# An encoder's step from out-projection to feed-forward: other h buffers, gate and up operands made earlier

## The chip, the cores and the metric

The kernel runs on one core of one Trainium2 chip. The metric is the device time of one execution in microseconds (us). The engines are TensorE (PE in the rows; PEld is its weight load), VectorE (DVE), ScalarE (ACT), GpSimd (POOL) and SyncE (SP), whose queue issues most of the DMAs.

## The reference

One layer of an encoder, for a prompt of 1024 tokens and a sample of 256, all in float32, with D = 1024 and a feed-forward width of 2816:

```python
x = x + token_mixer(rms_norm(x, norm_mix_g), w_in, ..., w_out)       # Fourier mixing and latent attention, then @ w_out
x = x + (silu(n @ w_gate) * (n @ w_up)) @ w_down   # n = rms_norm(x, norm_ffn_g)
return rms_norm(x, final_norm_g)
```

## The kernel before, in words

Activations lie transposed, features on the partitions. The 1280 tokens are three chunks: t = 0 and t = 1 (512 prompt tokens each) and t = 2 (the 256 of the sample). Each float32 operand of a product is split into a high and a low part: ScalarE makes the high one by a rounding copy (line 93), and a subtraction on DVE or POOL makes the low one (line 98). One block product is then three matmuls (`mm3`, line 112). All engines but SP run the instructions in the order in which the code is written; SP's DMAs are placed by a scheduler.

The stage around the change has two parts.

The **out-projection** (`out_proj`) multiplies the mixed heads by `w_out`, eight blocks m = 0..7 of 128 output features. For t < 2 a block is 48 matmuls of 256 columns, for t = 2 it is 24. A first loop does t = 0 beside the last of the attention. A second loop does t = 1 in step m and t = 2 two steps later. After each block DVE adds the residual (line 1100: the sum h), ScalarE squares it (1081), and POOL adds up the squares (1082, `hacc`). When a chunk is through, `Rstd` makes 1/rms: `pre` splits `hacc` (`ssq`; ScalarE and DVE), `mid` sums over the partitions by two matmuls with ones (188, 189) and takes Ln and Exp on ScalarE (197, 199), `post` refines in four DVE steps (208 to 215; the first is `var`, the last gives `rstd`). `scaled` then multiplies h by gain and rstd (1111: c). The sum h of t < 2 is kept in four `h` tiles, each for two blocks m and both chunks, and is stored to DRAM after t = 1. Tiles of the tag "w" (nine buffers of 8 KB a partition) hold h, split weights (`whl`), split gate and up operands (`wo`) and others.

The **feed-forward** multiplies pairs of 128-feature blocks of `w_gate` and `w_up` with the two prompt chunks by a seven-product scheme (Strassen's). The weight side has four plain blocks (A11, A12, A21, A22) and four sums (S1 to S4). The chunk side has B11 and B21 (from t = 0), B22 and T3 (from t = 1 alone at first), and the combinations T1, T2, T3, T4. `prep(upto)` makes the next weight-side pieces in the order of the list `seq`, and `run(n)` does product n: 24 matmuls. `rest(n)` multiplies a plain piece with the sample chunk: 12 matmuls. For the first pair (fp = 0) the order of `seq` is A11, A12, A21, A22 for gate and up (n = 0 to 7), then S2, S1, S3, S4 and A22 again (n = 8 to 17). Of the plain pieces, A11 and A12 are also multiplied with prompt chunks, as run(0) to run(3). From fp = 1 on the order is a steady one.

In `before` the calls stand so: after the second loop `prep(4)`, run(0), run(1); post of chunk 1 and eight `scaled`; pre of chunk 2; run(2); mid of chunk 2; `prep(8)`; the T1, T2, T4 combinations; run(3); the `rest` products; the later runs, each with its `prep` and `split_block` ahead of it. All low parts of gate and up pieces are POOL's.

Of the kernel before, what the change touches and what calls it, by code (L numbers as in the profile page):

```python
# [35 lines left out]
def encoder_kernel(ctx, tc, A, out):  # L36
# [22 lines left out]
    def wtile(shape, dt, s="w"):  # L59
        return sb.tile(shape, dt, tag="w", bufs=n_w, name=nm(s))  # L60
# [1006 lines left out]
    def hview(m, t):  # L1067
        if (m, t) in HV:
            return HV[m, t]
        if t < 2:  # L1070
            return Ha[m // 2][:, m % 2, t * 512 : (t + 1) * 512]
        return Hb[0][:, m, :]

    def square_sum(acc, m, t):
# [11 lines left out]
    def load_res(m, t):  # L1086
        t0, n = TC[t]
        xres[m, t] = araw([P, n])
        nc.sync.dma_start(xres[m, t], A["x"][m * P : (m + 1) * P, t0 : t0 + n])

    def out_proj(w, m, t):
        n = TC[t][1]
        b = bank()
        for c in range(8):
            mm3(b[:, :n], (w[:, 0, c * P : (c + 1) * P], w[:, 1, c * P : (c + 1) * P]), MX[c, t], c == 0, c == 7)
        if t == 0 and m % 2 == 0:
            Ha[m // 2] = wtile([P, 2, 1024], F32, "h")
        elif t == 2 and m == 0:
            Hb[0] = wtile([P, 8, 256], F32, "hb")
        nc.vector.tensor_tensor(hview(m, t), b[:, :n], xres.pop((m, t)), op=ALU.add)  # L1100
        square_sum(hacc, m, t)
        if t == 1:
            nc.sync.dma_start(hd[m], Ha[m // 2][:, m % 2, :])
        elif t == 2 and m == 7:
            nc.sync.dma_start(hd2, Hb[0])

# [52 lines left out]
    for m in range(10):
        W.split(min(io + 8 + m + 2, idn))  # L1160
        if m < 8:
            load_res(m + 1, 1) if m < 7 else None
            out_proj(W.get(io + 8 + m), m, 1)
        if m == 7:
            hch[1] = Rstd(hacc[1], 512, D)
            hch[1].pre()
        if m > 0 and m < 9:
            load_res(m - 1, 2)
        if m == 9:
            hch[1].mid()  # L1170
        if m > 1:
            out_proj(W.get(io + 6 + m), m - 2, 2)
            plain2(m - 2)
        if m == 0:
            hch[0].mid()
            hch[0].post()
        elif m < 5:
            chunk0(m - 1)
            chunk0(m + 3)
        for k in {4: (0,), 5: (1,), 6: (2, 3), 7: (4,), 8: (5, 6), 9: (7,)}.get(m, ()):  # L1180
            parts0(k)
# [17 lines left out]
    def prep(upto):  # L1199


        while done[0] < min(upto, len(seq)):
            n = done[0]
            fp, k, name = seq[n]
            q = 2 * fp + k
            load_pair(q)
            ra, rb = raws2[q]
            blk = {"A11": ra[:, :512], "A12": ra[:, 512:], "A21": rb[:, :512], "A22": rb[:, 512:]}
            blk |= {"S3": blk["A11"], "S1": blk["A21"], "S4": blk["A12"], "S2": sums.get(q)}
            eng = nc.vector if fp else nc.gpsimd  # L1210
# [26 lines left out]
    def rest(n):  # L1237

        fp, k, name = seq[n]
        if name not in FIRST:  # L1240
            return
        st, L = state[fp, k], piece[n]
        if name == "A11":
            st["G"] = bank()
        i, h = int(name[1]) - 1, int(name[2]) - 1
        R = [HN[4 * h + j, 2] for j in range(4)]

        block_product(st["G"][:, i * 256 : (i + 1) * 256], L, R, name == "A11", i == 1 or h == 1, i == 1)
        if name == "A22":
            g = st["2"] = tmp([P, 2, 256])  # L1250
# [112 lines left out]
    split_block("T3", nc.vector)
    run(8)
    run(9)
    split_block("B22", nc.vector)
# [251 lines left out]
```

## Time and the profile before

| | us |
|---|---|
| median of 3 runs (1469.0 to 1472.6) | 1472.11 |
| the profiled execution's own time | 1468.22 |
| its span, first to last instruction | 1466.4 |
| TensorE busy | 1405.7 (96%) |
| DVE, POOL, ACT busy | 851.7, 638.8, 558.7 |

The profile is of one execution, so its parts add up to 1466.4 and not to the median. A busy TensorE may still run at a lower clock: the granted clock (1.00 is 2.4 GHz, 0.50 is 1.2 GHz) has a column of its own in the view of stretches.

### The profile page before, as it was taken

How to read it: one execution, taken by the hardware profiler on the slowest of the kernel's cores; microseconds unless marked ns; L12 is line 12 of the kernel's file. 1: busy time of each engine (PE TensorE's matmuls, PEld its weight loads, DVE VectorE, ACT ScalarE, POOL GpSimd, SP SyncE). 2: the span in 40 equal slices, each digit the busy share in tenths (PEclk: the TensorE clock that was granted, in tenths of full speed). 3: DMA queues.
4: the chain of work that ended last, by engine and by line, in shares of the span. 5: the costliest groups of instructions: out<-in, count | busy, mean ns of one | idle time of the engine just before them, and what ended most of it. 6: DMA issues, size and time to landing. Idle time of an engine off the chain costs nothing.

```text
span 1466.4 us, 27581 instructions
## 1 busy us (share of the span) xinstructions
PE 1405.7 (96%) x11096; PEld 1357.0 (93%) x11096; DVE 851.7 (58%) x1279; ACT 558.7 (38%) x1115; POOL 638.8 (44%) x456
## 2 busy tenths in 40 slices
PE   9998899999989998889999999999999999999996
PEld 8898797888879998789999999999999999999996
DVE  6867947898994755863243324333432467777334
ACT  5544346776763433532222221222123331112134
POOL 3456514453552555664435443434343142325233
PEclk9999999999999998999999999999999999999998
DMA  8103445686764562031212122212222552243012
GB/s 261 50 1 118 135 130 131 152 201 171 187 187 118 180 201 85 8 114 47 78 66 92 47 72 74 83 48 73 80 74 93 176 166 84 85 149 135 1 43 103
DMA packets 75041, 157.51 MB, mean 107 GB/s; under 512 B 13088, under 2 KB 23072, under 8 KB 74784
## 3 DMA queue, kind: packets, MB, share of 16 engines
q1 hardware_dynamic: 71856, 150.74, 33.8%
q10 hardware_dynamic: 2736, 3.95, 0.7%
q8 instruction: 87, 1.43, 0.4%
q0 software_dynamic: 320, 1.05, 0.2%
q14 instruction: 42, 0.34, 0.1%
HBM read 99.57 MB, written 35.16 MB: 92 GB/s over the span
## 4 chain that ended last, share of the span: by engine, by line
PE 80%; DVE 7%; issue 3%; ACT 2%; POOL 2%; DMA 1%; SPq 1%; DVEq 0%; ACTq 0%; POOLq 0%
PE mm L112 50%; PE sc L112 23%; PE sc L744 1%; PE sc L745 1%; PE sc L748 1%; PE sc L747 1%; PE sc L746 1%; DVE b L98 1%; DVE mx L755 1%; DVE c L1338 1%; PE mm L821 1%; DVE pt L98 1%; SPq L805 0%; POOL wo L98 0%; DVE at L98 0%
## 5 line engine op out<-in xcount | busy, mean ns | idle before, releaser
L112 PE MATMUL sc<-b,wo 128*128 128x256 f32 x2288 | 299.2, 282 | 15.8 <-ACT wo L93 7.7
L112 PE MATMUL mm<-at,whl 128*128 128x256 f32 x2640 | 304.9, 277 | 4.6 <-DVE h L1412 2.3
L112 PEld LDWEIGHTS mm<-at,whl 128*128 128x128 f32 x2640 | 302.8, 188 | 6.0 <-DVE h L1412 2.9
L112 PEld LDWEIGHTS sc<-b,wo 128*128 128x128 f32 x2288 | 282.2, 193 | 17.3 <-ACT wo L93 8.3
L98 POOL TENSOR_TENSOR wo<-wraw,wo 128x512 fp32r<-128x512 f32 x156 | 211.8, 1380 | 160.2 <-ACT wo L93 160.1
L1269 DVE TENSOR_TENSOR e<-e,sc 128x512 f32<-128x512 f32 x64 | 44.0, 688 | 223.6 <-PE sc L112 223.6
L1412 DVE TENSOR_TENSOR h<-h,mm 128x512 f32<-128x512 f32 (+1 forms) x192 | 111.7, 595 | 102.6 <-PE mm L112 101.9
L98 POOL TENSOR_TENSOR whl<-wraw,whl 128x1024 fp32r<-128x1024 f32 (+3 forms) x49 | 117.5, 2410 | 89.5 <-ACT whl L93 78.2
L112 PE MATMUL mm<-hn,wo 128*128 128x256 f32 x1056 | 130.3, 277 | 0.0
L112 PE MATMUL mm<-b,wo 128*128 128x256 f32 x1056 | 127.1, 276 | 0.6 <-POOL wo L98 0.6
L112 PEld LDWEIGHTS mm<-hn,wo 128*128 128x128 f32 x1056 | 125.0, 188 | 0.0
L112 PEld LDWEIGHTS mm<-b,wo 128*128 128x128 f32 x1056 | 123.1, 188 | 1.0 <-POOL wo L98 0.8
L112 PEld LDWEIGHTS mm<-mx,whl 128*128 128x128 f32 x960 | 112.8, 189 | 2.3 <-POOL whl L98 1.5
L112 PE MATMUL mm<-mx,whl 128*128 128x256 f32 x960 | 113.6, 279 | 1.1 <-POOL whl L98 0.9
L93 ACT ACTIVATE at<-araw 128x512 fp32r<-128x512 f32 x55 | 32.9, 625 | 161.2 <-DMA araw<-a 97.8
L93 ACT ACTIVATE wo<-wraw 128x512 fp32r<-128x512 f32 x156 | 87.8, 619 | 10.1 <-POOL wraw L1213 5.7
L112 PE MATMUL mm<-pt,vt 128*128 128x512 f32 (+1 forms) x324 | 84.8, 398 | 4.3 <-DVE pt L98 3.9
L98 POOL TENSOR_TENSOR wo<-tmp,wo 128x512 fp32r<-128x512 f32 x22 | 29.2, 1325 | 132.8 <-ACT wo L93 132.8
L1425 POOL TENSOR_TENSOR h<-h,araw 128x512 f32<-128x512 f32 (+1 forms) x24 | 27.4, 1147 | 136.0 <-DVE h L1412 90.8
L98 POOL TENSOR_TENSOR pt<-wraw,pt 128x512 fp32r<-128x512 f32 x40 | 60.1, 1502 | 51.1 <-ACT pt L93 40.9
L1082 POOL TENSOR_TENSOR hacc<-hacc,tmp 128x512 f32<-128x512 f32 (+1 forms) x35 | 42.8, 1223 | 84.0 <-ACT tmp L1081 80.6
L112 PE MATMUL mm<-cn,whl 128*128 128x256 f32 x585 | 73.6, 282 | 5.2 <-DVE qw L581 3.2
(198 smaller groups left out, 2277.9 us busy)
## 6 DMA issues: line engine op xcount, KB each, us to landing
Y<-P SPq DMA_DIRECT2D x160, 128.0 KB, 2.5
wraw<-in_w_gate SPq DMA_DIRECT2D x22, 512.0 KB, 3.7
wraw<-in_w_up SPq DMA_DIRECT2D x22, 512.0 KB, 4.1
wraw<-in_w_down SPq DMA_DIRECT2D x22, 512.0 KB, 3.7
araw<-a SPq DMA_DIRECT2D x44, 256.0 KB, 4.6
a<-e SPq DMA_DIRECT2D x42, 256.0 KB, 2.0
araw<-in_x SPq DMA_DIRECT2D x32, 256.0 KB, 4.6
wraw<-in_w_out SPq DMA_DIRECT2D x16, 512.0 KB, 3.7
```

What stands on the lines that cost most here:

```text
L93: nc.scalar.activation(o, i, AF.Copy)
L98: eng.tensor_tensor(o, i, f(hi), op=ALU.subtract)
L112: nc.tensor.matmul(o[:, c], L[a], R[b][:, c], start=first and i == 0 and j == 0, stop=end, skip_group_check=again)
L744: nc.tensor.matmul(o, qn[0][:, cs], k[0], start=True, stop=False)
L745: nc.tensor.matmul(o, qn[0][:, cs], k[1], start=False, stop=False)
L746: nc.tensor.matmul(o, qn[1][:, cs], k[0], start=False, stop=False)
L747: nc.tensor.matmul(o, qr[0][:, cs], krst[kt], start=False, stop=False)
L748: nc.tensor.matmul(o, qr[1][:, cs], krst[kt], start=False, stop=True)
L1082: nc.gpsimd.tensor_tensor(acc[t], acc[t], q, op=ALU.add)
L1269: add = lambda o, x, y: nc.vector.tensor_tensor(o, x, y, op=ALU.add)
L1412: nc.vector.tensor_tensor(hview(m, t), hview(m, t), o, op=ALU.add)
L1425: nc.gpsimd.tensor_tensor(HV[m, t], HV[m, t], hres.pop((m, t)), op=ALU.add)
```

## The change

The sum h of t < 2 gets one tile for four blocks m of one chunk, and each block is stored as soon as it is added, 16 stores of 256 KB for eight of 512 KB. The second loop does t = 2 one step after t = 1, splits `w_out` one block further ahead, and makes the first pair's eight plain gate and up pieces in its steps 6 and 7; their low parts are DVE's. The first sums of the gate weights (S3, S1, S2, now S4 too) stand in step 7 on POOL. The rest is written in another order, the T4 differences move to POOL, and ScalarE loads the table set with Ln and Exp right after the feed-forward loop.

```diff
-            Ha[m // 2] = wtile([P, 2, 1024], F32, "h")
+        if t < 2 and m % 4 == 0:
+            Ha[t, m // 4] = wtile([P, 4, 512], F32, "h")
...
-        if t == 1:
-            nc.sync.dma_start(hd[m], Ha[m // 2][:, m % 2, :])
+        if t < 2:
+            nc.sync.dma_start(hd[m][:, t * 512 : (t + 1) * 512], hview(m, t))
...
-            if name == "S2":
+            if name == "S2" and q not in sums:
                 made("S3", "A11", "A21", ALU.subtract)
                 made("S1", "A21", "A22", ALU.add)
                 blk["S2"] = sums[q] = tmp([P, 512])
                 made("S2", "A22", "S3", ALU.subtract)
+                if fp == 0:
+                    made("S4", "A12", "S2", ALU.subtract)
...
-            piece[n] = split((o[:, 0], o[:, 1]), blk[name], nc.gpsimd)
+            piece[n] = split((o[:, 0], o[:, 1]), blk[name], nc.gpsimd if n > 7 else nc.vector)
...
+    LNEXP = "natural_log_exp_and_others"
+    for m in range(9):
+        W.split(min(io + 8 + m + 3, idn))
+        if m == 6:
+            prep(4)
+        if m == 7:
+            prep(8)
+        if m < 8:
+            load_res(m + 1, 1) if m < 7 else None
+            load_res(m, 2)
+            out_proj(W.get(io + 8 + m), m, 1)
+        if m == 7:
+            hch[1] = Rstd(hacc[1], 512, D)
+            hch[1].pre()
+            prep(9, True)
+        if m == 8:
+            hch[1].mid()
+        if m > 0:
+            out_proj(W.get(io + 7 + m), m - 1, 2)
+            plain2(m - 1)
...
+        for k in {4: (0,), 5: (1,), 6: (2,), 7: (3, 4, 5, 6, 7)}.get(m, ()):
+            parts0(k)
+        if m == 5:
+            load_pair(0)
+            load_pair(1)
+    hch[1].post()
...
-    prep(4)
     run(0)
-    run(1)
-    hch[1].post()
     for j in range(4):
         B["T3"][j], B["B22"][j] = low(vtile([P, 512], F32, "c")), low(vtile([P, 512], F32, "c"))
         scaled(B["T3"][j][1], j, 1)
         scaled(B["B22"][j][1], j + 4, 1)
+    run(1)
     hch[2] = Rstd(hacc[2], 256, D)
     hch[2].out = r2
     hch[2].pre()
-    run(2)
-    hch[2].mid()
-    prep(8)
+    prep(10)
...
-        combine(t4r[:, j], C0.pop(j + 4), B["T2"][j][1])
+        nc.gpsimd.tensor_tensor(t4r[:, j], C0.pop(j + 4), B["T2"][j][1], op=ALU.subtract)
+    hch[2].mid()
+    run(2)
+    run(3)
     split_block("T2", nc.vector)
-    run(3)
...
+    nc.scalar.preload_act_table_set(LNEXP)
```

On TensorE, the place is where the sum of squares of chunk 2 is taken (lines 188, 189); `sc` are the accumulators of gate and up, `wo` the weight pieces, b the chunk-side parts. Before:

```order
L112 MATMUL sc_7235<-b_7159,wo_7230 128x256 x2
L112 MATMUL sc_7235<-b_7158,wo_7230 128x256 x2
L188 MATMUL mm_7340<-ssq_7311,ones_r 128x256
L189 MATMUL mm_7340<-ssq_7311,ones_r 128x256
L112 MATMUL sc_7262<-b_7072,wo_7230 128x256 x2
```

And with the change:

```order
L112 MATMUL sc_7307<-b_7199,wo_6987 128x256 x2
L112 MATMUL sc_7307<-b_7198,wo_6987 128x256 x2
L188 MATMUL mm_7365<-ssq_7334,ones_r 128x256
L189 MATMUL mm_7365<-ssq_7334,ones_r 128x256
L112 MATMUL sc_7264<-b_7202,wo_6992 128x256 x2
```

Before, the pair stood behind run(2); now it stands behind run(1), 24 matmuls earlier.

On ScalarE, the place is the Ln of chunk 1 (line 197) at the end of the out-projection. Before:

```order
L93 ACTIVATE b_7072<-c_6479 128x512
L1081 ACTIVATE tmp_7104<-hb_6569 128x256
L95 ACTIVATE hn_7107<-hb_6569,gains 128x256
L93 ACTIVATE b_7110<-c_6578 128x512
L93 ACTIVATE b_7114<-c_6677 128x512
L197 ACTIVATE ln_7121<-mm_7118,eps 128x512
```

And with the change:

```order
L1081 ACTIVATE tmp_7192<-hb_6571 128x256
L95 ACTIVATE hn_7195<-hb_6571,gains 128x256
L93 ACTIVATE b_7198<-c_6874 128x512
L93 ACTIVATE b_7202<-c_6580 128x512
L93 ACTIVATE b_7206<-c_6679 128x512
L93 ACTIVATE b_7210<-c_6778 128x512
L93 ACTIVATE b_7214<-c_6876 128x512
L197 ACTIVATE ln_7221<-mm_7218,eps 128x512
```

Five copies of chunk-0 parts now stand in one block ahead of the Ln.

On POOL, the place is the end of the out-projection: `hacc` of 256 columns is chunk 2's, b are B21's low parts. Before:

```order
L1082 TENSOR_TENSOR hacc_6571<-hacc_6571,tmp_7104 128x256
L98 TENSOR_TENSOR b_7111<-c_6578,b_7110 128x512
L98 TENSOR_TENSOR b_7115<-c_6677,b_7114 128x512
L1082 TENSOR_TENSOR hacc_6571<-hacc_6571,tmp_7151 128x256
L98 TENSOR_TENSOR b_7159<-c_6776,b_7158 128x512
L98 TENSOR_TENSOR wo_7225<-wraw_7217,wo_7225 128x512
L98 TENSOR_TENSOR wo_7225<-wraw_7221,wo_7225 128x512
```

And with the change:

```order
L1189 TENSOR_TENSOR tmp_7163<-wraw_6981,wraw_6979 128x512
L1189 TENSOR_TENSOR wraw_6979<-wraw_6979,tmp_7163 128x512
L1082 TENSOR_TENSOR hacc_6573<-hacc_6573,tmp_7192 128x256
L98 TENSOR_TENSOR b_7203<-c_6580,b_7202 128x512
L98 TENSOR_TENSOR b_7207<-c_6679,b_7206 128x512
L98 TENSOR_TENSOR b_7211<-c_6778,b_7210 128x512
L98 TENSOR_TENSOR b_7215<-c_6876,b_7214 128x512
L1082 TENSOR_TENSOR hacc_6573<-hacc_6573,tmp_7251 128x256
L98 TENSOR_TENSOR wo_7337<-tmp_7163,wo_7337 128x512
L1189 TENSOR_TENSOR wraw_6983<-wraw_6983,wraw_6985 128x512
```

The gate's four sums and all four B21 parts now stand ahead of chunk 2's last `hacc`; the plain `wo` parts are gone from this queue.

## Rows read from the trace of the kernel before

**Rows 1.** Stretches: us, busy us of each engine (instructions), granted clock, DMA share, GB/s
```profile
505.00:567.00 62.00, 61.07 (x517) 60.79 (x516) 31.59 (x38) 20.06 (x34) 30.01 (x18) 1.00 0.54 171
567.00:648.00 81.00, 64.54 (x465) 62.56 (x463) 64.25 (x76) 37.72 (x67) 54.77 (x36) 0.85 0.15 49
672.00:800.00 128.00, 128.00 (x1125) 128.00 (x1125) 48.90 (x68) 32.64 (x59) 55.39 (x42) 1.00 0.21 73
```

**Rows 2.** TensorE's timeline: start, us, instructions, count, [idle before, who ended it]
```profile
508.27 59.16 PE L112 MATMUL mm<-mx,whl 128*128 128x256 f32 x500 [0.93 <-POOL whl L98]
567.27 0.40 PE L188 MATMUL mm<-ssq,ones_r 128*128 128x512 f32 x1
...
573.39 1.22 PE L112 MATMUL sc<-b,wo 128*128 128x256 f32 x4 [2.76 <-ACT wo L93]
576.91 10.83 PE L112 MATMUL sc<-b,wo 128*128 128x256 f32 x68 [2.30 <-POOL wo L98]
...
605.20 0.74 PE L112 MATMUL sc<-b,wo 128*128 128x256 f32 x4 [3.63 <-ACT wo L93]
...
628.73 8.24 PE L112 MATMUL sc<-b,wo 128*128 128x256 f32 x48 [4.36 <-DVE e L1269]
...
647.95 3.06 PE L112 MATMUL sc<-b,wo 128*128 128x256 f32 x24
```

**Rows 3.** Stretches of 2 us as in rows 1, after TensorE's idle time
```profile
577.00:579.00 2.00, 2.00 (x10) 2.00 (x11) 1.96 (x2) 0.00 (x0) 2.00 (x2) 0.50 0.00 0
...
581.00:583.00 2.00, 2.00 (x11) 2.00 (x11) 2.00 (x2) 0.60 (x1) 0.92 (x1) 0.51 0.00 0
583.00:585.00 2.00, 2.00 (x20) 2.00 (x19) 2.00 (x4) 0.00 (x0) 0.00 (x0) 1.00 0.00 0
```

**Rows 4.** DVE's timeline from the last sum of chunk 1
```profile
561.82 0.69 DVE L1100 TENSOR_TENSOR h<-mm,araw 128x512 f32<-128x512 f32 x1 [2.35 <-PE mm L112]
565.36 0.69 DVE L98 TENSOR_TENSOR ssq<-hacc,ssq 128x512 fp32r<-128x512 f32 x1 [2.85 <-ACT ssq L93]
...
572.77 0.68 DVE L208 TENSOR_SCALAR var<-mm 128x512 f32<-128x512 f32 x1
...
577.43 8.35 DVE L1111 SCALAR_TENSOR_TENSOR c<-h,gains,rstd 128x512 f32<-128x512 f32 x8
585.99 0.43 DVE L98 TENSOR_TENSOR ssq<-hacc,ssq 128x256 fp32r<-128x256 f32 x1 [0.20 <-ACT ssq L93]
586.33 1.41 DVE L1338 TENSOR_TENSOR c<-c,c 128x512 f32<-128x512 f32 x2
...
596.51 6.85 DVE L98 TENSOR_TENSOR b<-c,b 128x512 fp32r<-128x512 f32 x4
```

**Rows 5.** POOL's timeline
```profile
563.37 1.28 POOL L1082 TENSOR_TENSOR hacc<-hacc,tmp 128x512 f32<-128x512 f32 x1 [5.39 <-ACT tmp L1081]
567.04 0.74 POOL L1082 TENSOR_TENSOR hacc<-hacc,tmp 128x256 f32<-128x256 f32 x1 [2.38 <-ACT tmp L1081]
...
575.14 6.77 POOL L98 TENSOR_TENSOR wo<-wraw,wo 128x512 fp32r<-128x512 f32 x4
592.49 6.96 POOL L98 TENSOR_TENSOR wo<-wraw,wo 128x512 fp32r<-128x512 f32 x4 [10.57 <-ACT wo L93]
```

**Rows 6.** ScalarE's timeline
```profile
570.26 0.66 ACT L197 ACTIVATE ln<-mm,eps 128x512 f32<-128x512 f32 x1
...
585.54 0.41 ACT L93 ACTIVATE ssq<-hacc 128x256 fp32r<-128x256 f32 x1
...
593.88 4.27 ACT L93 ACTIVATE b<-c 128x512 fp32r<-128x512 f32 x8
```

**Rows 7.** DMA issues of the page: KB each, us from issue to landing
```profile
araw<-in_x SPq DMA_DIRECT2D x32, 256.0 KB, 4.6
```

**Rows 8.** TensorE's timeline at its last matmuls
```profile
1453.77 0.70 PE L1521 MATMUL mm<-sq,ones_r 128*128 128x256 f32 x2 [0.53 <-ACT sq L1504]
```

**Rows 9.** The chain that ended last, near its end: start, us, what
```profile
1453.74 1.28 ACT L197
...
1455.03 0.47 ACT ln L197
...
1455.53 1.28 ACT L199
```

More of the change, by code (lines that the diff above doesn't have):

```diff
@@ L1070, in hview @@
         if t < 2:
-            return Ha[m // 2][:, m % 2, t * 512 : (t + 1) * 512]
+            return Ha[t, m // 4][:, m % 4]
         return Hb[0][:, m, :]
@@ L1095, in out_proj @@
             mm3(b[:, :n], (w[:, 0, c * P : (c + 1) * P], w[:, 1, c * P : (c + 1) * P]), MX[c, t], c == 0, c == 7)
-        if t == 0 and m % 2 == 0:
-            Ha[m // 2] = wtile([P, 2, 1024], F32, "h")
+        if t < 2 and m % 4 == 0:
+            Ha[t, m // 4] = wtile([P, 4, 512], F32, "h")
         elif t == 2 and m == 0:
@@ L1158, in encoder_kernel @@
     hch[0].pre()
[L1159 to L1181, printed above, removed]
     NB = NF // 2
@@ L1197, in load_pair, with prep @@
             raws2[q] = [wload(src[f_ * P : (f_ + 1) * P, :], 1024) for f_ in (q // 2 * 2, q // 2 * 2 + 1)]
-    def prep(upto):
+    def prep(upto, only_sums=False):
         while done[0] < min(upto, len(seq)):
@@ L1219, in prep @@
                 made("S2", "A22", "S3", ALU.subtract)
-            elif name == "S4":
+                blk["S2"] = sums[q]
+                if fp == 0:
+                    made("S4", "A12", "S2", ALU.subtract)
+            elif name == "S4" and fp:
                 made("S4", "A12", "S2", ALU.subtract)
+            if only_sums:
+                return
             if n % 2 == 0:
@@ L1249, in rest @@
         if name == "A22":
-            g = st["2"] = tmp([P, 2, 256])
+            g = st["2"] = (tmp if fp else vtile)([P, 2, 256], F32)
             r = hch[2].r.rearrange("p (o n) -> p o n", o=1).broadcast_to([P, 2, 256])
@@ L1317, in run @@
             finish("21", ad[fb, 0])
-    load_pair(0)
-    load_pair(1)
-    prep(4)
+    LNEXP = "natural_log_exp_and_others"
[18 more added lines that the diff above has]
+            plain2(m - 1)
+        if m == 0:
+            hch[0].mid()
+            hch[0].post()
+        elif m < 5:
+            chunk0(m - 1)
+            chunk0(m + 3)
+        for k in {4: (0,), 5: (1,), 6: (2,), 7: (3, 4, 5, 6, 7)}.get(m, ()):
[4 more added lines that the diff above has]
+    hch[1].post()
     run(0)
-    run(1)
-    hch[1].post()
     for j in range(4):
@@ L1332, in encoder_kernel @@
     hch[2].pre()
-    run(2)
-    hch[2].mid()
-    prep(8)
+    prep(10)
     def combine(o, x, y):
         nc.vector.tensor_tensor(o, x, y, op=ALU.subtract)
-    t4, t4r = wtile([P, 4, 512], F32R, "t4"), wtile([P, 4, 512], F32, "t4r")
     for j in range(4):
@@ L1346, in encoder_kernel @@
         combine(B["T2"][j][1], cb, B["T1"][j][1])
+    t4, t4r = wtile([P, 4, 512], F32R, "t4"), wtile([P, 4, 512], F32, "t4r")
+    for j in range(4):
         B["T4"][j] = (t4[:, j], t4r[:, j])
-        combine(t4r[:, j], C0.pop(j + 4), B["T2"][j][1])
+        nc.gpsimd.tensor_tensor(t4r[:, j], C0.pop(j + 4), B["T2"][j][1], op=ALU.subtract)
+    hch[2].mid()
+    run(2)
+    run(3)
     split_block("T2", nc.vector)
-    run(3)
     hch[2].post()
-    rest(0)
-    rest(2)
+    prep(12)
+    for n in (0, 2, 4, 6):
+        rest(n)
     split_block("T1", nc.vector)
-    rest(1)
-    rest(3)
-    prep(10)
+    for n in (1, 3, 5, 7):
+        rest(n)
+    run(8)
+    run(9)
     for j in range(4):
         combine(B["T3"][j][1], B["B22"][j][1], B["T3"][j][1])
-    for n in range(4, 8):
-        rest(n)
+    split_block("T3", nc.vector)
     prep(14)
[L1363 to L1366, printed above, removed]
     run(10)
     run(11)
+    split_block("B22", nc.vector)
+    prep(18)
+    run(12)
+    run(13)
     split_block("T4", nc.vector)
-    for n in range(12, len(seq)):
+    for n in range(14, len(seq)):
         prep(n + 6)
```

## The prediction

> **What bounds the kernel now.** I read the stretches first. From 672 us on TensorE is busy in the whole of every stretch: 1125 matmuls in 128.00 us, 0.1138 us each, the pace that I use for all 256-column matmuls below [rows 1]. During the second loop of the out-projection it is busy 61.07 of 62 us. Between these, from 567 to 648 us, it is busy only 64.54 of 81 us, at a granted clock of 0.85 [rows 1]. The change works in that stretch, so its gain must come from there.
>
> TensorE's timeline tells what that stretch loses. From the sum of squares at 567.27 to the start of fp = 1 at 647.95 are 80.7 us [rows 2]. The work in it is one out-projection block (24 matmuls), fourteen runs (336) and eight rests (96): 456 matmuls, 51.9 us, and 52.6 with the four small ones-matmuls. So 28.1 us are lost. Some are waits (2.76, 2.30, 3.63, 4.36 and smaller ones [rows 2]); the rest is the clock: after the waits before 576.91 the granted clock is 0.50 (1.2 GHz), with 10 or 11 matmuls in 2 us, and at 583 it is 1.00 (2.4 GHz) again, with 20 [rows 3]. The waits name gate and up pieces (`wo`) and DVE's sums.
>
> Last I read DVE and POOL side by side. While both work from SBUF they take turns: four low parts on DVE take 6.85 us, while four on POOL take 6.96 [rows 4, 5], 1.72 us for a pair. DVE alone takes 0.70 (two in 1.41 [rows 4]), POOL alone 1.28 [rows 5]. The eight `scaled` fit: POOL works until 581.91 [rows 5], which gives DVE 2.6 of them in 4.5 us, and 5.4 at 0.70 make 8.3 us; they took 8.35 [rows 4].
>
> **The change, part by part.** *Eight plain low parts, POOL to DVE, and their copies.* They leave the bad stretch (8 at 1.74 on POOL, 13.9 us) for steps 6 and 7 of the second loop, where DVE is busy 31.59 and ScalarE 20.06 of 62 us, and TensorE never waits [rows 1]. They cost 8 x 0.70 = 5.6 us of DVE and, at 4.27/8 = 0.53 [rows 6], 4.3 us of ScalarE; idle time hides both. Their loads follow splits that stand one step earlier. Should they be late, TensorE waits 5.1 us before run(0) and run(1) as now (2.76 + 2.30 [rows 2]), which the wait below would swallow. I take 0.
>
> *Stores of h.* SP's queue now waits for DVE's sum of block m ahead of the loads for step m + 1. These then start some 7 us later, land in 4.6 us [rows 7], and are used a step (near 8 us) later. I take 0; the cover is that one step, and each microsecond beyond it would be one of ScalarE's. More splitting ahead: 0, POOL is busy 30.01 of 62 us [rows 1].
>
> *Mid of chunk 1.* Only one block of 24 now lies between block (7, t = 1) and the ones-matmuls; before there were two. That block's product ends at 561.8, when its sum starts [rows 4]; with the other block ahead of it (500 matmuls in 59.0 us [rows 2], 2.8 us) at 564.6. From the sum to the end of `ssq` before: 561.82 to 566.05, 4.2 us [rows 4]. So 568.8, and POOL's first sum, which now follows `hacc` at once, can hold DVE 0.4 longer: 569.2. TensorE arrives at 567.3, as now: **1.9 us** (1.4 to 2.2). The last block and runs 0 and 1 then end at 577.7 (0.5 + 3 x 2.73 later).
>
> *Mid of chunk 2, ahead of run(2).* TensorE runs in order, so it stops at 577.7 until DVE's low half of chunk 2's `ssq` is there, with run(2) to run(17) and the rests queued behind it. That half stands behind `rstd` of chunk 1 and eight `scaled`. On ScalarE, a square, an `hn` copy and five b copies (5 x 0.53) precede the Ln from 569.6 on: Ln at 573.3 for 570.26 [rows 6]. `var` came 2.5 us behind it [rows 4, 6]; with a POOL turn in between I put it at 576.3. POOL has, from 567.2 on, four sums, four B21 parts and two small `hacc` (0.74 [rows 5]): 11.7 us alone, and 0.44 for each of the seven DVE instructions that take turns with it, until 582. By then DVE has finished `rstd` (three turns). ScalarE's half of `ssq` (0.41 [rows 6]) and a copy follow, during which DVE is alone and does two `scaled`, to 583.7. Then POOL has six more for the sums, so six `scaled` take 6 x 1.72 = 10.3, and `ssq` 0.43 [rows 4]: 594.5. **16.8 us**. From below: no turns at all, 576.3 + 12 x 0.70 + 0.43 = 585.1, 7.4 us; from above: turns throughout, 577.0 + 11 x 1.72 + 0.43, and waiting for a last POOL instruction, near 597, 19 us. I take 16.8, since POOL's list is full then.
>
> *Clock.* After so long an idle time TensorE starts at 0.50, as at 577: some 32 matmuls in 6 us for 3.6 [rows 3]: **2.4 us**, with nearly the same at either bound.
>
> *Later waits.* Runs 2, 3 and the rests (144 matmuls, 16.4 us + 2.4) end at 613.3. DVE by then: eight combinations with POOL's four T4 differences (to 604), four T2 parts in turns (610.5): in time. T1 by 615.6 for run(10) at 618.8. T3 waits in DVE's order for run(9)'s sum: 619.5, four combinations (2.8), four parts at 0.70 to 1.72: some 1 us late for run(12) at 624.2. B22 by 634, some 1.5 late for run(14); T4 some 0.5. **3.0 us** (0 to 6).
>
> *Table load after the feed-forward loop.* At the end two loads of 1.28 us stand on the chain before and after Ln [rows 9]. Without them Ln follows TensorE's end (1453.77 + 0.70 [rows 8]) at 1454.5, and Exp at 1455.0 for 1456.8: **1.8 us** saved. The load itself lies where TensorE has work.
>
> **The sum.** Lost after: 1.9 + 16.8 + 2.4 + 3.0 = 24.1 for 28.1: 4.0 gained, with the end 5.8. The profiled execution's 1468.2 would become 1462.4; the median of the runs stands 3.9 above it: 1472.1 - 5.8 = 1466.3. With all bounds good the loss is 11 and the time 1453, with all bad 29.8 and 1472.
>
> **Rivals.** *Short wait* (0.17): DVE hardly meets POOL and `ssq` is there near 585.1; 9.4 more gained, 1457. For it: 0.70 a piece at 586. Against it: POOL's queue has ten instructions there, and it paused at 582 to 592 before only because ScalarE's copies were late [rows 5], which the change removes.
>
> *Nothing gained between DVE and POOL* (0.20): work that changes sides between two engines that take turns gives nothing; the wait before run(2), at 19, and later waits of 6 eat what the stretch gained, and only the end's 1.8 stays: 1470.3. For it: the turns [rows 4, 5], and that four T4 differences go the other way. Against it: the eight parts go to a stretch where POOL leaves the port free half the time [rows 1]. A rule beside it: the Trainium skill (Perfetto Trace Analysis, "Optimizing Scalar/DVE Operations") says that the two share an SBUF read port, so that offloading between them might not help. By that rule the time is this rival's; the trace agrees on the turns.
>
> *Slower* (0.08): the waits before runs 12 to 17 are long enough to drop the clock, and these 144 matmuls go at 0.50: 2/10.7 = 0.187 us each, 10.6 us more: 1476.9. It decides whether a wait there is like the 3.63 us before 605.2, after which the clock was low, or like the 0.93 at 508.27, after which it was not [rows 2].
>
> **How the numbers follow.** My forecast (0.55) is 1466, its own range 1462 to 1471. About 0.3% (4.4 us) is what a measurement of this kernel can tell from no change: three quarters of the forecast lie beyond it. Faster: 0.41 + 0.17 = 0.58; within: 0.14 + 0.20 = 0.34; slower: 0.08. The range 1457 to 1472 leaves out half of the short wait and the slower case.
>
> **What would show it.** Right: no wait for `wo` before run(0); one wait of 15 to 19 us on DVE's `ssq` before run(2), `scaled` at 1.7 us beside POOL, clock 0.50 after it; no table load near the end. Wrong: `ssq` before 590, waits for `whl` in the out-projection, or waits over 3 us before runs 8 to 17.

## The result, and the profile after

The changed kernel takes 1460.1 us (median of 6 runs, 1457.6 to 1462.9), the kernel before 1469.2 us (6 runs, 1465.1 to 1472.6): a ratio of 0.9939, 95% interval 0.9918 to 0.9961. The gain is 9.2 us by the medians, beyond the 0.3% that can be told from no change; the forecast was 1466 and a gain of 5.8. In a second comparison on one chip the changed kernel stood at 1462.2 and the kernel before at 1469.9, 7.6 us, ratio 0.9948 (0.9925 to 0.9970).

The profiled execution has a span of 1455.3 us and a time of 1457.6, against 1466.4 and 1468.2. These 11.1 us are more than the change gives, as will be seen.

Stretches of the changed kernel; the first two answer to [rows 1], the last four to [rows 3]:

```profile
505.00:567.00 62.00, 59.85 (x521) 59.06 (x519) 40.25 (x46) 24.08 (x41) 32.22 (x21) 1.00 0.43 140
567.00:648.00 81.00, 64.12 (x520) 63.02 (x521) 67.46 (x76) 34.52 (x63) 52.72 (x35) 0.89 0.16 56
577.00:579.00 2.00, 0.00 (x0) 0.00 (x0) 1.93 (x3) 0.00 (x0) 2.00 (x2) 1.00 0.00 0
...
593.00:595.00 2.00, 2.00 (x12) 2.00 (x11) 2.00 (x2) 0.83 (x1) 1.37 (x2) 0.50 0.04 8
595.00:597.00 2.00, 2.00 (x12) 2.00 (x12) 1.97 (x3) 0.27 (x1) 1.37 (x2) 0.60 0.00 0
597.00:599.00 2.00, 2.00 (x20) 2.00 (x19) 1.97 (x2) 1.88 (x4) 1.60 (x1) 1.00 0.00 0
```

In the same 81 us TensorE's records number 520 where there were 465, and DVE, which took work over, is busier. The reader is to see two things in the short stretches: while TensorE waits, DVE is busy without a pause, and after the wait the granted clock is 0.50 (1.2 GHz) for some 6 us before it is 1.00 (2.4 GHz) again.

TensorE's timeline, which answers to [rows 2]:

```profile
508.33 56.95 PE L112 MATMUL mm<-mx,whl 128*128 128x256 f32 x500 [0.93 <-POOL whl L98]
566.15 0.49 PE L188 MATMUL mm<-ssq,ones_r 128*128 128x512 f32 x1 [0.87 <-ACT ssq L93]
567.27 0.50 PE L189 MATMUL mm<-ssq,ones_r 128*128 128x512 f32 x1 [0.62 <-DVE ssq L98]
567.60 2.99 PE L112 MATMUL mm<-mx,whl 128*128 128x256 f32 x24
570.43 5.82 PE L112 MATMUL sc<-b,wo 128*128 128x256 f32 x48
579.87 0.58 PE L188 MATMUL mm<-ssq,ones_r 128*128 128x256 f32 x1 [3.62 <-ACT ssq L93]
590.99 0.58 PE L189 MATMUL mm<-ssq,ones_r 128*128 128x256 f32 x1 [10.53 <-DVE ssq L98]
591.37 8.09 PE L112 MATMUL sc<-b,wo 128*128 128x256 f32 x48
599.29 11.04 PE L112 MATMUL mm<-hn,wo 128*128 128x256 f32 x96
610.17 5.60 PE L112 MATMUL sc<-b,wo 128*128 128x256 f32 x48
...
622.51 3.01 PE L112 MATMUL sc<-b,wo 128*128 128x256 f32 x24 [0.85 <-POOL wo L98]
626.11 2.56 PE L112 MATMUL sc<-b,wo 128*128 128x256 f32 x20 [0.58 <-POOL wo L98]
...
640.80 3.07 PE L112 MATMUL sc<-b,wo 128*128 128x256 f32 x24 [1.01 <-DVE e L1250]
```

The two waits for gate and up pieces before run(0) and run(1), and with them the slow clock there, are gone. One long wait, 3.62 + 10.53 us on chunk 2's `ssq`, has come in ahead of run(2), and runs 2 and 3 take 8.09 us instead of the 5.60 of runs 8 and 9. The last row is the start of fp = 1, at 640.80 for 647.95.

DVE and then POOL in that wait, to be read beside [rows 4, 5]:

```profile
573.66 0.68 DVE L208 TENSOR_SCALAR var<-mm 128x512 f32<-128x512 f32 x1
...
577.15 1.63 DVE L215 SCALAR_TENSOR_TENSOR rstd<-ln,r 128x512 f32<-128x512 f32 x1
578.82 11.77 DVE L1111 SCALAR_TENSOR_TENSOR c<-h,gains,rstd 128x512 f32<-128x512 f32 x8
590.52 0.41 DVE L98 TENSOR_TENSOR ssq<-hacc,ssq 128x256 fp32r<-128x256 f32 x1
590.86 8.29 DVE L1347 TENSOR_TENSOR c<-c,c 128x512 f32<-128x512 f32 x8
...
600.16 4.90 DVE L98 TENSOR_TENSOR b<-c,b 128x512 fp32r<-128x512 f32 x4
```

```profile
578.20 1.17 POOL L1082 TENSOR_TENSOR hacc<-hacc,tmp 128x256 f32<-128x256 f32 x1
...
583.45 1.59 POOL L1189 TENSOR_TENSOR wraw<-wraw 128x512 f32<-128x512 f32 x1
585.00 1.71 POOL L1189 TENSOR_TENSOR tmp<-wraw,wraw 128x512 f32<-128x512 f32 x1
...
620.24 11.28 POOL L98 TENSOR_TENSOR wo<-wraw,wo 128x512 fp32r<-128x512 f32 x6 [16.32 <-ACT wo L93]
```

POOL's last `hacc` is done at 579.4, but the low half of `ssq`, which needs 0.41 us, starts at 590.52: it stands behind eight `scaled`. Their mean is 1.47 us, which mixes two lengths: six of them, with POOL's sums of 1.59 to 1.71 beside them, take 1.75 us each, the other two 1.09 and 0.74; the combinations of [rows 4] took 0.70 with POOL idle. At 600.16 DVE makes T2's four parts (done at 605.06), which run(8) needs.

ScalarE at the end, to be read beside [rows 8, 9]:

```profile
1444.34 0.42 ACT L1518 ACTIVATE sq<-h 128x256 f32<-128x256 f32 x1 [1.28 <-DVE h L1426]
1445.55 0.47 ACT L197 ACTIVATE ln<-mm,eps 128x256 f32<-128x256 f32 x1 [0.79 <-PE mm L1535]
1446.06 0.42 ACT L199 ACTIVATE r<-ln 128x256 f32<-128x256 f32 x1
```

No table load stands there. From the start of the last square to the end of Exp it takes 2.14 us, where it took 3.93 (1453.31 to 1457.24).

### The profile page after: what moved, and what is told of

Its sections match the earlier page's. It is cut to its first block, busy times and chain, and to the rows that moved or that the text cites. A ratio compares the mean times of both kernels' runs of the same rounds, so it can differ in the third digit from the quotient of the medians.

```text
span 1455.3 us, 27581 instructions
## 1 busy us (share of the span) xinstructions
PE 1395.1 (96%) x11096; PEld 1346.9 (93%) x11096; DVE 858.9 (59%) x1283; ACT 549.3 (38%) x1107; POOL 633.4 (44%) x452
## 4 chain that ended last, share of the span: by engine, by line
PE 80%; DVE 8%; issue 2%; ACT 2%; DMA 2%; POOL 1%; SPq 0%; DVEq 0%; ACTq 0%; POOLq 0%
PE mm L112 50%; PE sc L112 23%; PE sc L744 1%; PE sc L745 1%; PE sc L748 1%; PE sc L747 1%; PE sc L746 1%; DVE c L1111 1%; DVE mx L755 1%; DVE mx L98 1%; PE mm L821 1%; POOL whl L98 1%; DMA Y<-P 1%; DVE qw L581 0%; DVE at L98 0%
## 5 line engine op out<-in xcount | busy, mean ns | idle before, releaser
L112 PE MATMUL sc<-b,wo 128*128 128x256 f32 x2288 | 292.0, 278 | 2.4 <-POOL wo L98 1.4
L112 PEld LDWEIGHTS sc<-b,wo 128*128 128x128 f32 x2288 | 275.9, 189 | 3.0 <-POOL wo L98 1.8
L98 POOL TENSOR_TENSOR wo<-wraw,wo 128x512 fp32r<-128x512 f32 x148 | 201.2, 1382 | 155.4 <-ACT wo L93 155.4
```

Source lines behind the costliest of these rows:

```text
L98: eng.tensor_tensor(o, i, f(hi), op=ALU.subtract)
L112: nc.tensor.matmul(o[:, c], L[a], R[b][:, c], start=first and i == 0 and j == 0, stop=end, skip_group_check=again)
```

## The experiments

Two measures are used. The runs of one kernel spread over 5 to 16 us, so that 2 us are hardly told by them. The trace tells more: what lies from the end of the out-projection's 500 matmuls (the row with x500) to the start of fp = 1 is here called the **stretch**. The kernel before has 80.5 us and, profiled once more, 81.0; the changed kernel 75.5, 74.4 and, without the table load, 75.4, so 80.7 and 75.1 on average (here and below, *the changed kernel's average* is that of its three profiles). One profile stands for each of the other kernels, so that differences of 1 us in the table are within this spread.

The whole stretch of the kernel before, and below it that of the changed kernel, in the columns of [rows 1]:

```profile
567.43:647.95 80.52, 64.06 (x462) 62.08 (x460) 64.15 (x76) 37.24 (x66) 54.33 (x36) 0.85 0.15 50
565.28:640.80 75.52, 57.42 (x461) 56.01 (x461) 64.48 (x74) 30.95 (x57) 48.46 (x32) 0.89 0.15 53
```

TensorE is not idle for less time after the change: 18.1 us (75.52 - 57.42), where it was 16.5 (80.52 - 64.06), and 15.9 in the second profile of the kernel before. What became shorter is its busy time for the same matmuls, 57.0 us for 64.6 on average. Before, several waits each had matmuls at a lower granted clock behind them: 0.50 from 577 to 583 [rows 3] and again from 607 to 609, 0.59 from 613 to 617, 0.50 from 629 to 633. Now only the long wait has. The table gives the idle time beside the stretch; the rest of the stretch is busy time.

| kernel | stretch, us | TensorE idle in it, us | TensorE's wait for chunk 2's ssq, us | T2 done, us after the 500 | median, us | ratio to the kernel before (95%) |
|---|---|---|---|---|---|---|
| changed, again | 74.4 | 18.2 | 14.7 | 39.7 | 1462.2 | 0.9948 (0.9925 to 0.9970) |
| ssq first | 73.7 | 11.5 | 3.7 | 40.6 | 1460.2 | 0.9944 (0.9924 to 0.9965) |
| mid late | 73.2 | 12.3 | 0.7 | 39.9 | 1458.0 | 0.9928 (0.9899 to 0.9956) |
| no sums | 69.1 | 12.4 | 8.9 | 33.6 | 1457.2 | 0.9921 (0.9894 to 0.9948) |
| low parts on POOL | 76.6 | 18.5 | 14.5 | 40.4 | 1461.4 | 0.9945 (0.9924 to 0.9966) |
| sums on DVE | 71.0 | 14.0 | 10.3 | 38.7 | 1458.2 | 0.9926 (0.9898 to 0.9954) |
| sums early | 78.6 | 20.1 | 7.4 | 42.9 | 1464.4 | 0.9967 (0.9945 to 0.9989) |
| sums early, ssq first | 77.6 | 17.4 | 1.1 | 44.5 | 1463.7 | 0.9965 (0.9943 to 0.9988) |
| sums in idle time | 72.6 | 15.6 | 11.6 | 37.1 | 1460.6 | 0.9940 (0.9915 to 0.9964) |
| sums in idle time, ssq first | 69.5 | 10.5 | 5.8 | 37.0 | 1456.7 | 0.9893 (0.9855 to 0.9931) |
| no preload | 75.4 | 18.1 | 14.2 | 39.8 | 1464.2 | 0.9960 (0.9937 to 0.9983) |

The first four were timed on one chip, the other seven on another, in two batches; each ratio is to runs of the kernel before from the same batch. In the changed kernel's own first profile T2 is done 39.8 us after the 500 matmuls.

**Changed kernel and kernel before, again.** No edit.

> The changed kernel once more, nothing edited. In the first profile of it the 500 matmuls ahead of the first ones-matmul of chunk 1 took 56.95 us, 0.1139 each, in the kernel before 59.16 us, 0.1183 each, both at a granted clock of 1.00. Theory: this pace differs from execution to execution and is no gain of the change; the profiled 11.1 us between the two spans hold some 3 us of it, and the runs' 9 us less or none. Then this profile shows another figure than 56.95, or the kernel before profiled again another than 59.16. Rival: the change quickens these matmuls (eight fewer POOL splits near them, other stores); then 57.0 again here and 59.2 again there. The wait before run(2) should be 14 to 16 us again by either, and the ratio to the kernel before within 0.992 to 0.996.

> The kernel before, profiled once more. The changed kernel's 500 matmuls of the out-projection took 56.95 us in one profile and 59.16 in the other, with nothing edited; the kernel before showed 59.16. Theory: one of two paces falls to an execution whatever the kernel, so 56.95 or 59.16 here, and the stretch from their end to fp = 1 again 80 to 81 us (79 with the quicker pace). Rival: the kernel before always shows 59.2.

TensorE's row of the 500 matmuls, of the changed kernel again, and below it of the kernel before again:

```profile
511.23 59.16 PE L112 MATMUL mm<-mx,whl 128*128 128x256 f32 x500 [0.74 <-POOL whl L98]
```

```profile
512.20 56.95 PE L112 MATMUL mm<-mx,whl 128*128 128x256 f32 x500 [0.93 <-POOL whl L98]
```

The two figures have changed sides. So the 2.2 us by which the out-projection was quicker in the first profile are no gain of the change, and the stretch is measured from their end. One execution says little by its total: this one of the changed kernel took 1469.4 us, more than the 1468.2 of the kernel before, though its stretch is 6 us shorter.

**The low half of ssq first.** TensorE's order stays, on DVE one instruction passes eight:

```
     run(0)
+    run(1)
+    hch[2] = Rstd(hacc[2], 256, D)
+    hch[2].out = r2
+    hch[2].pre()
     for j in range(4):
...
         scaled(B["B22"][j][1], j + 4, 1)
-    run(1)
-    hch[2] = Rstd(hacc[2], 256, D)
-    hch[2].out = r2
-    hch[2].pre()
```

> DVE's low half of chunk 2's ssq stands ahead of the eight scaled, nothing else is moved. Theory of the prediction (the wait before run(2) is DVE's order: ssq behind eight scaled): POOL's last hacc ends at 579.4 and ScalarE's half at 579.8, so ssq at 580.3; TensorE waits 4 us instead of 14.9, and run(2), run(3) and the rests end near 599 to 600 instead of 610.2. Then T2 is late: DVE's chain is 1.2 later than now, its four parts end at 606 instead of 605.1, run(8) starts on the first of them near 602.5: a new wait of 2 to 4 us, and fp = 1 starts 5 to 8 us sooner; time 5 to 8 us below the changed kernel, ratio near 0.989. Rival A (the chain scaled, combinations, T2 bounds the stretch, and run(8) waits for the last part of T2 at 606 with all that follows at the same distances): 3 to 4 us sooner. Rival B (POOL's hacc or ScalarE is what is late, not DVE's order): the wait stays above 12 us, no change.

TensorE in this run:

```profile
588.66 0.38 PE L188 MATMUL mm<-ssq,ones_r 128*128 128x256 f32 x1 [3.65 <-ACT ssq L93]
...
589.35 7.23 PE L112 MATMUL sc<-b,wo 128*128 128x256 f32 x48
596.41 11.04 PE L112 MATMUL mm<-hn,wo 128*128 128x256 f32 x96
607.29 0.39 PE L112 MATMUL sc<-b,wo 128*128 128x256 f32 x2
610.75 8.71 PE L112 MATMUL sc<-b,wo 128*128 128x256 f32 x46 [3.07 <-DVE b L98]
...
626.99 1.22 PE L112 MATMUL sc<-b,wo 128*128 128x256 f32 x4 [2.08 <-ACT wo L93]
629.28 7.36 PE L112 MATMUL sc<-b,wo 128*128 128x256 f32 x44 [1.08 <-POOL wo L98]
```

The wait is 10.5 us shorter, so it was indeed DVE's order that held TensorE (rival B falls). But 500 matmuls end at 574.05 here, and counted from there the rests are done at 33 us instead of 45, T2 at 40.6 instead of 39.8. TensorE now waits for T2 (3.07, and 8.71 us for 46 matmuls, where 48 take 5.60) and again before and in runs 12 and 13. Of the 10.5 us, 1.4 are left in the stretch: less than the theory said, and less than rival A. The expectation of 5 to 8 was wrong. The rest is lost in two places. Run(10) still starts 4.7 us sooner than the changed kernel's average, counted from the 500, near the 5.1 by which T2 was early there; run(14) only 0.4, since run(12)'s `wo` piece is late. And it is lost in two ways: TensorE is idle for 6.6 us less and busy for 5.2 us more, as new waits bring the clock of 0.50 with them (46 matmuls in 8.71 us, 44 in 7.36).

**Mid of chunk 2 late.** DVE's order stays, TensorE goes on with what it has:

```
-    hch[2].mid()
     run(2)
     run(3)
     split_block("T2", nc.vector)
-    hch[2].post()
     prep(12)
-    for n in (0, 2, 4, 6):
-        rest(n)
+    for n in (0, 2, 4, 1, 3, 5):
+        rest(n)
+    hch[2].mid()
+    hch[2].post()
+    rest(6)
     split_block("T1", nc.vector)
-    for n in (1, 3, 5, 7):
-        rest(n)
+    rest(7)
```

> DVE's order as in the changed kernel, but TensorE's ones-matmuls of chunk 2, and with them Ln, Exp and rstd of chunk 2, stand behind run(2), run(3) and six of the eight rests; only the last two products of the rests' gate and up need them. Theory: TensorE works from 576 to 590 on runs 2, 3 and six rests, waits 1 us or less for ssq at 591, keeps its clock, and stands with the last two rests done at 594 to 595, where it now would at 610; then it waits for T2, whose parts come from 601.4 to 605.1 as now: a wait of 6 to 8 us before run(8) in place of 14.9 before run(2), and runs 8 and on 5 to 8 us sooner, the same as with ssq first. Rival A: run(8) waits for the whole of T2 and rstd of chunk 2 delays T1, 3 us sooner at most. Rival: the G products, now late, hold DVE's T1 parts, and the gain is nothing.

```profile
571.79 11.49 PE L112 MATMUL sc<-b,wo 128*128 128x256 f32 x96
583.12 8.64 PE L112 MATMUL mm<-hn,wo 128*128 128x256 f32 x72
...
602.67 8.97 PE L112 MATMUL sc<-b,wo 128*128 128x256 f32 x46 [6.63 <-DVE b L98]
```

This is the other way to take the wait away, and it ends at the same place: no wait ahead of run(2), no lower clock there, but 6.63 us before run(8), then a granted clock of 0.50 and 8.97 us for 46 matmuls. The stretch is 1.9 us shorter, not 5 to 8. Two quite different edits meet at the same moment, T2 done some 40 us after the 500: DVE's chain of `rstd`, `scaled`, combinations and T2 stands right behind the wait that the profile names. Behind T2 stands run(12)'s piece, here too: run(10) starts 5.1 us sooner than the changed kernel's average, run(14) 0.8, after waits of 1.82 and 1.54 us and 44 matmuls in 7.64.

**No sums.** The edit skips the eight adds and subtractions of the first pair in `prep`.

> The first pair's eight weight sums are left out (S1, S2, S3 and S4 of its gate and up take plain blocks, so its products are not the reference's); everything else stands as in the changed kernel. It takes eight POOL instructions of 1.28 us away, of which seven to eight meet DVE's. Theory (turns between DVE and POOL stretch DVE's chain): scaled at about 0.70 each but for those that meet the two low parts and hacc, ssq done near 585 instead of 590.9, the wait before run(2) 8 to 10 us, T2 done 6 to 8 us sooner, and the time 6 to 8 us below the changed kernel. Rival (DVE's instructions have their length from something else, or ssq waits for POOL's hacc): scaled stay at 1.4 to 1.5, less than 2 us gained.

DVE in this run:

```profile
581.49 7.40 DVE L1111 SCALAR_TENSOR_TENSOR c<-h,gains,rstd 128x512 f32<-128x512 f32 x8
588.82 0.41 DVE L98 TENSOR_TENSOR ssq<-hacc,ssq 128x256 fp32r<-128x256 f32 x1
```

The eight `scaled` take 7.40 us instead of 11.77, with DVE's own instructions untouched; T2 is done 6.2 us sooner and the stretch is 6.0 us shorter. The trace is as expected: taking turns with POOL's sums costs this much. It goes to the end through `ssq`, for which TensorE waits 5.3 to 5.8 us less; T2 comes before TensorE needs it, here as in the changed kernel. By the medians the gain is 5.0 where 6 to 8 was expected, and the two intervals overlap.

**Low parts on POOL.** `split(..., nc.gpsimd if n > 7 else nc.vector)` becomes `split(..., nc.gpsimd)`.

> The eight plain low parts stay in steps 6 and 7 of the out-projection, but on POOL as in the kernel before instead of DVE. It tells apart what the move to an earlier place gives and what the move to another engine gives. Stretch measured from the end of the 500 matmuls of the out-projection to the start of fp = 1: 80.5 us in the kernel before, 75.5 and 74.4 in the changed one. Theory (it is the place in time: POOL has the idle time in these steps, 8 x 1.28 to 1.74 = 10 to 14 us more there): the last four come behind four others and ahead of block (7, t = 1)'s hacc, so they end near 565 and delay the ssq of chunk 1 by 0 to 3 us; stretch 75 to 78. Rival (it is the engine: POOL's queue is full, its parts slip behind 567 into the stretch and hold the four gate sums, B21 parts and hacc): POOL is 8 to 14 us later in the stretch and so are ssq and T2; stretch 80 to 86, no better than the kernel before.

The stretch is 76.6, 1.5 more than the changed kernel's average and 4.1 less than the kernel before: 0.6 us of the 1.5 are a longer wait for ScalarE's half of chunk 1's `ssq` (1.45 for 0.87). So the other engine is worth 1.5 us at most, little above the spread, and 4.1 of the 5.6 us stay without it. That these are due to the earlier place fits the waits for `wo` that are gone; no run undoes that place alone, the new `h` tiles or the earlier t = 2, so how the 4.1 us divide among them is not shown.

**Sums on DVE.** `eng = nc.vector if fp else nc.gpsimd` becomes `eng = nc.vector`.

> The eight weight sums of the first pair are made by DVE instead of POOL, at the same places of the program. Stretch as above; leaving the sums out gave 69.1, the changed kernel 75.5 and 74.4. Theory (a POOL sum beside DVE's work costs DVE 0.7 to 1.0 us in turns, as much as DVE takes for it alone, so that which of the two makes it hardly matters): eight sums cost DVE 5.6 us, of which some 1 to 2 lie in idle time before var; scaled at 0.9 as without sums, T2 done within 2 us of the changed kernel; stretch 72 to 76. Rival (POOL's sums fill time that DVE needs, so DVE must get slower with them): T2 4 us later than in the changed kernel, stretch 78 to 80.

```profile
589.01 0.68 DVE L1189 TENSOR_TENSOR wraw<-wraw,wraw 128x512 f32<-128x512 f32 x1
...
591.66 9.29 DVE L1347 TENSOR_TENSOR c<-c,c 128x512 f32<-128x512 f32 x8
```

The busier engine takes eight instructions more, T2 comes 1.1 us sooner all the same, the wait ahead of run(2) is 4 us shorter, and the stretch is 71.0, below the range of either theory. T2 does not decide here: it is done 38.7 us after the 500 and TensorE comes to run(8) at 39.8, so that the shorter wait for `ssq` goes to the end whole. By the medians (1458.2, and 1460.1 to 1462.2 for the changed kernel) it cannot be told. A sum costs DVE 0.69 us when POOL is quiet; made by POOL it cost DVE about as much in turns (`ssq` came 6.2 us sooner without the eight), and TensorE more, since the turns lay ahead of `ssq`.

**Sums early, alone and with ssq first.** Both loads of the first pair and the eight plain parts one step earlier, and all sums on POOL at the start of step 7 (`early_sums(q)` makes S3, S1, S2 and S4 of the gate for q = 0, of the up for q = 1):

```
+        if m == 7:
+            early_sums(0)
+            early_sums(1)
...
-            prep(9, True)
```

> All eight sums stay on POOL but are made ahead of the out-projection's last block of chunk 1 (step 7 of the second loop), with the loads of the first pair and the eight plain parts one step earlier each; then POOL has only B21 parts, hacc and S2's low parts beside DVE's rstd and scaled. Theory (the turns with the sums cost the 5.3 to 6.4 us that leaving them out gave): the same here, stretch 69 to 71, wait before run(2) some 9 us, time 4 to 6 us below the changed kernel, if POOL has the 10.2 us in steps 6 and 7, where it was busy 32 of 62 us. Rival (POOL's late sums hold hacc of block (7, t = 1), or the loads a step earlier take slots from the out-projection's weights): TensorE waits 2 to 8 us more before the ones-matmuls of chunk 1 or for whl, and the stretch and what is ahead of it together come to the same as now.

> The sums early, as in the run beside it, and DVE's low half of chunk 2's ssq ahead of the eight scaled. With ssq first alone the wait went from 14.9 to 4.0 us before run(2), but 3.1 us came back before run(8) and more within it and before run(12), since DVE was busy without a pause from 588.7 to 629 there: stretch 73.7, at most 2 us gained. Theory (DVE's chain rstd, scaled, combinations, T2, T1 sets the stretch, and the sums' turns lengthen it by 4 to 5 us): together they gain more than either, as T2 comes 4 to 5 us sooner and TensorE has run(2), run(3) and the rests meanwhile; stretch 66 to 69, time 6 to 8 us below the changed kernel, ratio near 0.989. Rival (behind T2 it is POOL's low parts for run(12) and run(14) that end last): stretch as with the early sums alone.

```profile
578.14 0.80 PE L188 MATMUL mm<-ssq,ones_r 128*128 128x512 f32 x1 [10.21 <-ACT ssq L93]
```

The rival came true: ScalarE's copies for the last two plain parts wait until 559.8, by the trace on TensorE's matmuls (which fits a slot that the out-projection still reads; it was not tested apart), POOL starts its sums at 565.4, and `hacc` of block (7, t = 1), which stands behind all eight, comes at 576.2. The new wait of 10.21 us eats what the sums gave, and the stretch is 78.6, for 69 to 71 expected. With ssq first it is 77.6, for 66 to 69.

**Sums in DVE's idle time, alone and with ssq first.** The same `early_sums`, on DVE and at other places:

```
         if m == 7:
+            early_sums(0)
             hch[1] = Rstd(hacc[1], 512, D)
             hch[1].pre()
-            prep(9, True)
...
             out_proj(W.get(io + 7 + m), m - 1, 2)
+            if m == 8:
+                early_sums(1)
```

> All eight sums on DVE, at two places where its trace shows it idle: the gate's four behind the sum of block (7, t = 1), where DVE waits 2.84 us for ScalarE's half of ssq, and the up's four behind that of block (7, t = 2), where in the run with the sums on DVE it waited 2.88 us for the hn copy. Stretch from the end of the 500 matmuls to fp = 1: changed kernel 75.5 and 74.4, sums on DVE at the old places 71.0, sums left out 69.1. Theory (DVE's chain up to T2 sets the stretch, and here no sum is in it): as without the sums, 68.5 to 70.5, the wait before run(2) 8 to 9 us. Rival (the sums wait for the raw blocks or for ScalarE's copies of them and hold ssq of chunk 1 or hn): 2 us or more of new wait before the ones-matmuls of chunk 1, stretch 71 to 74.

> The same, and DVE's low half of chunk 2's ssq ahead of the eight scaled. Theory: with ssq first alone the wait before run(2) turned into waits before and within runs 8, 9 and 12, as T2 came no sooner (stretch 73.7); with T2 now 5 to 6 us sooner as well, TensorE finds most of it ready when the rests end, and the stretch is bound by DVE's work behind T2, 33 us in the run with ssq first: 66 to 68; time 6 to 9 us below the changed kernel, ratio to the kernel before 0.987 to 0.990. Rival (POOL's four pieces ahead of runs 12 to 15, behind T1 on ScalarE, end last whatever DVE does): stretch as with the sums in idle time alone, 69 or more.

DVE in the run with the sums alone, at the up's four:

```profile
572.99 0.68 DVE L1216 TENSOR_TENSOR wraw<-wraw,wraw 128x512 f32<-128x512 f32 x1
573.70 1.68 DVE L1217 TENSOR_TENSOR wraw<-wraw 128x512 f32<-128x512 f32 x1
575.30 1.78 DVE L1218 TENSOR_TENSOR tmp<-wraw,wraw 128x512 f32<-128x512 f32 x1
577.12 1.66 DVE L1219 TENSOR_TENSOR wraw<-wraw,tmp 128x512 f32<-128x512 f32 x1
```

Alone it gave 72.6, the rival's figure but not by the rival's cause: the waits before the ones-matmuls of chunk 1 are 1.9 us, where they were 1.5. DVE's idle time there is POOL's time for the B21 parts, and four sums took 5.8 us instead of 2.8. Together with ssq first the stretch is 69.5, 5.6 us shorter than the changed kernel's, though 1.5 above what was expected and within the rival's 69 or more. It has the lowest median of all, 1456.7, and a ratio of 0.9893; its interval still meets those of the changed kernel, so that the runs alone do not settle that it is faster than that kernel. In it run(12) waits 1.28 us for ScalarE's copy and 1.56 for POOL's low part, and the next 44 matmuls, the rest of it and run(13), take 6.92 us: these pieces are late next, as the rival had it. The first of POOL's six low parts there waits 13.5 us for the copy on ScalarE, which stands behind T3's in ScalarE's order. What moving them would give was not tried.

**No preload.** The line `nc.scalar.preload_act_table_set(LNEXP)` is taken out.

> The changed kernel without the table load behind the feed-forward loop. Theory: the 1.8 us at the end come back: two loads of 1.28 us stand before and behind the last Ln, from the start of the last square to the end of the last Exp 3.9 us instead of 2.1, and the span by the trace is otherwise as in the changed kernel. By the medians 1.8 us is less than can be told. Rival: ScalarE's loads in the down-projection move so that the last one lies elsewhere, and the end stays 2.1.

```profile
1447.49 0.42 ACT L1517 ACTIVATE sq<-h 128x256 f32<-128x256 f32 x1 [1.33 <-DVE h L1425]
1447.92 1.28 ACT L197 ACT_TABLE_LOAD   x1
...
1449.71 1.28 ACT L199 ACT_TABLE_LOAD   x1
1451.01 0.42 ACT L199 ACTIVATE r<-ln 128x256 f32<-128x256 f32 x1
```

3.94 us from square to Exp instead of 2.14, with the stretch unchanged at 75.4: the 1.8 us are the preload's.

## Why the prediction was right, and where its sizes were off

The direction, the range of 1457 to 1472 and the mechanism held; the forecast's own range, 1462 to 1471, did not hold the 1460.1. Of the 6.2 us between 1466.3 and 1460.1, 2.9 lie in where the sum began: 1472.1 was the median of three runs, and six gave 1469.2. By its own account, 52.6 us of work in the stretch, 28.1 us were lost before (80.7 - 52.6) and 22.5 after (75.1 - 52.6), for 24.1 forecast: 5.6 gained instead of 4.0. With the end's 1.8 the traces give 7.4; the medians gave 9.2 and 7.6. That 22.5 came so near to 24.1 is in part luck, as two misses cancel: the waits were put at 21.7 us and were 18.1, the longer busy time was put at 2.4 (the clock) and was 4.4 (57.0 - 52.6).

- **Eight plain low parts, stores of h, earlier splits: 0.** Right. No `wo` wait stands before run(0) or run(1), and TensorE has no new `whl` wait in the 500 matmuls.
- **Mid of chunk 1: 1.9.** Measured 0.87 + 0.62 = 1.5.
- **Mid of chunk 2: 16.8.** Right in place and cause, too long by 2.1 to 2.6: 14.2 and 14.7 were measured, under the 15 to 19 that were to show it right. The eight `scaled` were sized well (12.0 forecast, two alone and six in turns; 11.77 measured, with just these six in turns). Some 0.6 us are slips in the sum: 569.2 + 0.5 + 3 x 2.73 is 577.9 and not 577.7, and two `scaled` of 0.70 from 582 on end at 583.4 and not 583.7. The rest of the miss lies ahead of them: `rstd` was put at 14.7 us after the 500 matmuls and was done at 13.5, with Ln and `var` already 0.3 and 0.6 us sooner than put, and TensorE came to the wait 0.6 later (576.25, 11.0 after the 500, for 10.4). The bounds of 7.4 and 19 held the value. That DVE's order sets this wait was shown by ssq first, and what stretches it by no sums.
- **Clock: 2.4.** Runs 2 and 3 took 8.09 and, again, 7.07 us, where runs 8 and 9 took 5.60: 2.5 and 1.5. The other 2.2 to 2.3 us of longer busy time are in no term of the prediction; the four ones-matmuls alone, each beside a wait, took 2.2 us (0.49 + 0.50 + 0.58 + 0.58) where 0.7 was put.
- **Later waits: 3.0.** Measured 0.85 + 0.58 + 1.01 = 2.4, and 2.1 again. The place, run(12), was right; the wait ends on POOL's low part and not on DVE's T3 part, since ScalarE's copy of the piece stands behind T3's copies.
- **Table load: 1.8.** Right, and shown by itself.

The short wait did not come: `ssq` was done at 590.9, 25.6 us after the 500, when the rival wanted 585.1, 17.8 after them. The rival *nothing gained between DVE and POOL* was wrong about the whole, but half right in its premise: the same parts on POOL at the earlier place keep 4.1 of the 5.6. The Trainium skill (Perfetto Trace Analysis, "Optimizing Scalar/DVE Operations") says that moving work between the two might not help, as they share a read port. For the eight low parts the trace nearly agrees (1.5 us); for the sums it does not, as their move to DVE shortened the stretch by 4.1 us in one profile. The rival *slower* did not come: the waits before runs 12 to 17 stayed at 1 us and the clock at 1.00. What it describes does appear where those waits are longer: behind 2.08 + 1.08 us in ssq first and 1.82 + 1.54 in mid late the granted clock was 0.50, and 44 matmuls took 7.36 and 7.64 us, for 5.0 at the full pace of 0.1138 each.

What the prediction did not see is how little stood behind its largest term. It priced the wait ahead of run(2) at 16.8 and let one believe that this much was to be had there. Two runs took the wait away and kept 1.4 and 1.9. Nor does it say that the 21.7 us of waits that it forecast are more than the 16.5 for which TensorE was idle before: with these figures the whole gain had to come from the clock.

## What to carry to other kernels

When one wait dominates a stretch, look for the next operand that the waiting engine needs and ask when it would be there without the wait: here T2 was done 5 us before TensorE came for it, so that of the wait of 14 not much more than 5 could be had before run(10), and as run(12)'s piece was late next, less than 2 was at the end. Count the slow clock together with the waits: the changed kernel is idle for longer and still faster, as one long wait slowed its matmuls down once where several had done so again and again, and the two edits that cut some 6 us of idle time made the matmuls 4 to 5 us longer. Where two engines take turns, price an instruction by what it adds to the other's chain: eight POOL sums, which no wait of TensorE names, cost it 6 us by the one profile without them. Moving work into an engine's idle time was free here only where the engine that it takes turns with was idle too.

## What had not been expected of the hardware

The out-projection's 500 matmuls take 56.95 or 59.16 us at a granted clock of 1.00, 0.114 or 0.118 us each, and nothing between: of the fourteen profiles two show the longer time, one of the kernel before and one of the changed kernel, and each of these two kernels showed the shorter one as well. Later in the kernel 24 matmuls take 2.99 us in some places and 2.88 in others. What chooses the pace stays open. The start of the 500 matmuls lies between 508.3 and 517.1 us in the profiles of the changed kernel and those made from it, which differ only behind that place. From the start of fp = 1 to the end the changed kernel took 814.5 us in one profile and 822.4 in the other, with nothing edited. So the difference of two spans, one profile each, can be off by several microseconds, and here 11.1 us of spans stood for some 7.4.
